# Cross-attention memory keys and values: projected in the second norm of the mixer, or in the band heads of the next block

## The chip, the cores and the metric

One core of one Trainium2 chip runs the whole program. The metric is the device time of one execution in microseconds (us); the time of a version is the median of its runs. Engines are named as the profile names them: PE (TensorE matmuls), PEld (its weight loads), DVE (VectorE), ACT (ScalarE), POOL (GpSimd), SP (SyncE, which only issues DMAs here).

## The reference, cut to what matters

Two blocks follow each other on 512 positions of width 1024 (the first has 16 meta positions ahead of them). The first is a token mixer and a gated feed-forward; the second takes its output through four groups of heads (A dilated, B stick-breaking, C a band of 128 with a learned sink, D block-sparse), a cross-attention into 256 memory tokens, and a squared-ReLU feed-forward. All is float32. What the change touches:

```python
# first block
h = h + rmsnorm(merged @ w_out, g_post)                  # the mixer's second norm
h = rmsnorm(h, g_pre)                                    # channel_mixer
a = causal_dwconv(h @ w_gate, w_conv, b_conv)            # FFN_DIM = 2816
y = (gelu(a) * (h @ w_up)) @ w_down
# second block
x = x + concat(groups) @ w_out                           # hybrid_mixer: heads, then this
kv = rmsnorm_2(mem, g_mem) @ w_kv                        # mem: 256 x 1024, w_kv: 1024 x 512
p = softmax(einsum("bshe,bmhe->bhsm", q, k) * X_SCALE)   # q from x
o = einsum("bhsm,bmhe->bshe", p, v)
```

The memory is an input of its own: its keys and values depend on nothing that the first block computes, and are wanted only by the cross-attention.

## The kernel before, in words

**Products.** Activations lie transposed, eight tiles of 128 features by positions. Every number is held as a high and a low part of a reduced type, and a product is hi·hi + hi·lo + lo·hi: `mm3` (L141) and `product` (L160) issue three matmuls for each of eight 128-row slices, 24 for each range of columns. `weights` (L111) loads 512 KB of float32 through SP's queue into one of three buffers `wst`; ACT writes the high part `whi` (L126) and DVE the low part `wlo` (L127), three buffers each. `split_early` (L130) splits a weight ahead of time: a load on POOL's queue (L135), ACT and DVE for `phi` and `pst` (L105, L106), two stores to DRAM on POOL's queue (L139); `weights(..., ready=...)` then only loads both parts through SP (L119, L120).

**Banks.** `product_bank` (L185) gives accumulators in turn: in `merge` and in the feed-forward from three banks `mx` and two banks `mm`; in the heads from the two `mm` alone. A further bank `rs` is for the norms' factors.

**`merge` (L954)** runs the mixer's output product in two halves of the columns (`TAIL`), eight weights each. Between the eight outputs of the first half `memory_input` (L1582) loads the memory, splits it into tiles `ya`, `yb` that are free by then, and forms its norm's factor. Each half is followed by `post_norm` (L1034), a chain of twelve steps over DVE, ACT and POOL: a factor `prs`, then for each of eight tiles a multiply (L1039, in turn on DVE and on POOL), the residual sum (L1040), the split for the next product (L108, L109) and the square for the next norm (`add_square`, L243; its sums L252 are on POOL), and at its end the next norm's factor `rs` (L287 to L307). The first half's chain is woven between the second half's output products. The second half's chain, the *second norm*, has no output products left beside it, so `zip_steps` (L998) spreads the list `early` between its steps: the two key and two value products of the memory (`memory_keys`, L1602) and the products on the first half of the columns for three feed-forward weights (gate 0, up 0, gate 1), seven products of 24 matmuls with 256 or 258 columns:

```python
load, early = self.chain(self.memory_keys(mem), jobs[0][0])
early.insert(0, load)
jobs[0] = (lambda: None, jobs[0][1])
...
for load, pieces in jobs[0:3]:
    early += [load] + pieces[0:3]
    rest += pieces[3:]
```

Keys and values go to DRAM (`mkd`, `mvd`) by ten POOL DMAs (L1621, L1637) and come back in the cross-attention (`memory_load`, L1640).

**Feed-forward (`ffn_jobs` L1051, `ffn` L1088).** What `early` didn't take is `rest`: second halves, then the other gate and up products. A product's evacuation multiplies by `rs` (`graw` L1062, `up` L1077). Between the pieces seventeen `split_early` prepare weights of the second block.

**The second block's heads (`hybrid`, L1342).** `weave` (L1314) runs the chains of two pairs of heads side by side and puts the jobs of `plan` (L1527) between them: projections for later heads, and at the last two sets, the band heads ("C", 0) and ("C", 1), the first half of the output product: `project_out(f)` for eight f (L1510; 12 matmuls of 512 columns, a weight of 256 KB, and a sum into x). `finish(g)` turns a group's outputs into split inputs. The jobs of a set are placed in order among its units; each job's weight is loaded at the job before it.

**Order.** The framework reorders instructions by its own estimate of times; on the chip each engine, and each engine's DMA queue, takes its instructions in the order that the program then has.

The functions that the diff touches:

Of the kernel before, what the change touches and what calls it, by code (L numbers as in the profile page):

```python
# [11 lines left out]
FT = mybir.dt.float32  # L12
FR = mybir.dt.float32r
# [6 lines left out]
P = 128  # L20
# [43 lines left out]
class Net:  # L64
# [95 lines left out]
    def product(self, src, ranges, evac, m=P, after=None, own=None):  # L160

        nc = self.nc
        st = {}
# [19 lines left out]
        return load, pieces + ([after] if after else [])  # L183

# [769 lines left out]
    def merge(self, mem, mt, yas, ybs, mg, sgs):  # L954
# [93 lines left out]
    def ffn_jobs(self, e2):  # L1048
# [7 lines left out]
        for f in range(NFF):  # L1056
            t = {}

            def gate(ps, t0, n, t=t):
                if "g" not in t:  # L1060
                    t["g"] = ft.tile([P, L], FT, name="graw")
                V.tensor_tensor(t["g"][:, t0:t0 + n], ps, rs[:, t0:t0 + n], OP.mult)  # L1062
# [21 lines left out]
            jobs.append(self.product(I["w_gate"][f], TAIL, gate, after=conv))  # L1084
            jobs.append(self.product(I["w_up"][f], HALF if f < 2 else WHOLE, up, after=end))
        return jobs

    def ffn(self, e2, rest):  # L1088
        nc = self.nc
        I = self.I  # L1090
        with ExitStack() as es:
            self.fp = self.pool(es, "fp")
            self.hid = hid = []
            with ExitStack() as e3:
# [5 lines left out]
                early[11:11] = [("v", 2, c) for c in range(2)]  # L1100
                for i, piece in enumerate(rest):
                    piece()
                    while len(self.ready) < min(len(early), (i + 1) * len(early) // (len(rest) - 20)):
                        key = early[len(self.ready)]
                        self.split_early(pool, key, I["w_in2"][key[1]] if key[0] == "f" else I["w_v2"][key[1], key[2]])
# [236 lines left out]
    def hybrid(self):  # L1342
# [3 lines left out]
        with ExitStack() as es:  # L1346
# [165 lines left out]
            def project_out(f):  # L1512
# [13 lines left out]

            plan = [  # L1527
# [8 lines left out]
                (("C", 0), [(None, [lambda: finish(1), lambda: finish(0)])] + [project_out(f) for f in range(3)]),  # L1536
                (("C", 1), [(None, [lambda: finish(3)])] + [project_out(f) for f in range(3, 6)] + [
# [40 lines left out]
    def memory_input(self, mp):  # L1578
# [5 lines left out]
        self.mem = mh, ml, rm  # L1584
        for k in range(KT):
# [12 lines left out]
    def memory_keys(self, mp):  # L1598
# [3 lines left out]
        mh, ml, rm = self.mem  # L1602
        self.mkd = self.dram.tile([64, 8, MEM], FT, name="mkd")
        self.mvd = self.dram.tile([P, 4, 256], FT, name="mvd")

        def keys(f):
            st = {}

            def load():
                st["w"] = self.weights(I["w_xk"][f], (8, P))  # L1610

            def make():
                ps = self.product_bank()
                self.mm3(ps[:, 0:MEM], self.terms(st["w"], 0, list(zip(mh, ml)), 0, MEM, KT))
                kn = mp.tile([P, MEM], FT, name="kn")
                nc.vector.tensor_tensor(kn, ps[:, 0:MEM], rm, OP.mult)
# [354 lines left out]
```

## Time and profile before

| | |
|---|---|
| runs | 1526.29, 1524.48, 1523.43 us; median 1524.48 |
| profiled execution | 1522.43 us; span 1520.6 us from the first to the last instruction |
| busy in the span | PE 1464.7 us, DVE 1007.9, ACT 741.1, POOL 292.7 |
| mean granted clock of TensorE | 0.993 of full speed |
| DMA | 197.10 MB, mean 130 GB/s |

The span is 1.83 us shorter than its execution's own time. Landmarks of the span, by the lines that run: the second norm is at 441 to 480 us (the memory's products at 441 to 455), the feed-forward's gate and up products follow to about 770, the D heads end and the band heads run at 1000 to 1070, with the output products among them, and the cross-attention follows. A busy time is the sum over an engine's instructions, overlaps counted once; an engine that isn't busy in a stretch waits for another or for data.

### The profile page before, as it was taken

The page shows a single profiled execution, that of the slowest core. Times are in us where ns is not written, and L with a number is a line of the kernel's source. Part 1 is how long each engine was busy: PE and PEld are TensorE (multiplying, and loading weights), DVE is VectorE, ACT ScalarE, POOL GpSimd, SP SyncE. Part 2 cuts the span into 40 slices and gives each one's busy share as a digit, 9 for nine tenths or more (in the row PEclk, how much of TensorE's full clock was granted, in tenths as well). Part 3 has the DMA queues.
Part 4 walks back from the last instruction along what each step waited for, and adds up shares of the span by engine and source line. Part 5 has one row for each costly group of instructions (what it writes and reads, how often), then busy time and mean ns, then how long its engine had stood idle before and what let it go on. Part 6 is the DMA issues. An engine that isn't in the chain of part 4 may idle for free.

```text
span 1520.6 us, 25150 instructions
## 1 busy us (share of the span) xinstructions
PE 1464.7 (96%) x9769; PEld 1320.4 (87%) x9769; DVE 1007.9 (66%) x1963; ACT 741.1 (49%) x1437; POOL 292.7 (19%) x332
## 2 busy tenths in 40 slices
PE   7899899999999999999999999999899999999996
PEld 7899899988989989989999988888888888888885
DVE  6988979877587766655474766798895443344334
ACT  5333357665565444444454465686675431144321
POOL 1157822003363111100141221000221000000001
PEclk9999999999999999999999999999999999999998
DMA  6333332226545766643657344314311332232221
GB/s 207 100 100 95 107 113 77 77 68 224 161 151 199 245 242 224 246 140 116 189 154 244 106 142 138 112 46 143 98 56 58 96 97 97 89 96 94 97 84 56
DMA packets 75087, 197.10 MB, mean 130 GB/s; under 512 B 16076, under 2 KB 24508, under 8 KB 74840
## 3 DMA queue, kind: packets, MB, share of 16 engines
q1 hardware_dynamic: 65816, 165.08, 34.8%
q0 software_dynamic: 8064, 29.36, 5.4%
q8 instruction: 77, 1.26, 0.3%
q10 hardware_dynamic: 1088, 1.05, 0.2%
q14 instruction: 42, 0.34, 0.1%
HBM read 171.75 MB, written 27.63 MB: 131 GB/s over the span
## 4 chain that ended last, share of the span: by engine, by line
PE 62%; DVE 5%; ACT 2%; DMA 1%; issue 0%; DVEq 0%; ACTq 0%
PE mm L146 6%; PE mm L147 6%; PE mm L149 6%; PE mm L176 5%; PE mm L179 5%; PE mm L178 5%; PE mx L179 4%; PE mx L176 4%; PE mx L178 4%; PE mx L146 2%; PE mx L147 2%; PE mx L149 2%; PE mm L1396 2%; PE mm L1395 2%; PE mm L1393 2%; PE tr L1252 1%
## 5 line engine op out<-in xcount | busy, mean ns | idle before, releaser
L127 DVE TENSOR_TENSOR wlo<-wst,whi 128x1024 fp32r<-128x1024 f32 (+3 forms) x244 | 299.9, 1230 | 192.7 <-ACT whi L126 117.9
L126 ACT ACTIVATE whi<-wst 128x1024 fp32r<-128x1024 f32 (+3 forms) x244 | 249.9, 1026 | 269.7 <-PE mm L147 112.6
L178 PE MATMUL mm<-xh,whi 128*128 128x256 f32 (+4 forms) x784 | 225.6, 313 | 3.2 <-DVE u L762 2.1
L179 PE MATMUL mm<-xl,whi 128*128 128x256 f32 (+4 forms) x784 | 226.4, 314 | 0.3 <-DVE xl L109 0.2
L178 PE MATMUL mx<-xh,whi 128*128 128x512 f32 (+3 forms) x592 | 178.1, 324 | 7.4 <-ACT xh L108 7.2
L179 PE MATMUL mx<-xl,whi 128*128 128x512 f32 (+3 forms) x592 | 178.8, 325 | 0.6 <-DVE xl L109 0.6
L178 PEld LDWEIGHTS mm<-xh,whi 128*128 128x128 f32 (+1 forms) x784 | 148.1, 189 | 13.5 <-DVE u L762 2.5
L179 PEld LDWEIGHTS mm<-xl,whi 128*128 128x128 f32 (+1 forms) x784 | 147.7, 188 | 11.0 <-DVE xl L109 0.7
L176 PE MATMUL mm<-xh,wlo 128*128 128x256 f32 (+4 forms) x784 | 135.6, 312 | 0.6 <-DVE wlo L127 0.6
L146 PE MATMUL mm<-hh,whi 128*128 128x256 f32 (+1 forms) x480 | 132.7, 307 | 0.0
L147 PE MATMUL mm<-hl,whi 128*128 128x256 f32 (+1 forms) x480 | 132.6, 307 | 0.0
L178 PEld LDWEIGHTS mx<-xh,whi 128*128 128x128 f32 x592 | 112.1, 189 | 16.3 <-ACT xh L108 7.2
L176 PEld LDWEIGHTS mm<-xh,wlo 128*128 128x128 f32 (+1 forms) x784 | 113.1, 187 | 10.7 <-DVE wlo L127 0.8
L179 PEld LDWEIGHTS mx<-xl,whi 128*128 128x128 f32 x592 | 111.8, 189 | 10.7 <-DVE xl L109 1.5
L176 PE MATMUL mx<-xh,wlo 128*128 128x512 f32 (+3 forms) x592 | 107.5, 323 | 0.0
L176 PEld LDWEIGHTS mx<-xh,wlo 128*128 128x128 f32 x592 | 88.8, 189 | 9.0
L146 PEld LDWEIGHTS mm<-hh,whi 128*128 128x128 f32 x480 | 90.4, 189 | 5.4
L147 PEld LDWEIGHTS mm<-hl,whi 128*128 128x128 f32 x480 | 90.5, 189 | 5.1
L252 POOL TENSOR_TENSOR nacc<-nacc,sq 128x256 f32<-128x256 f32 (+2 forms) x58 | 56.4, 972 | 196.9 <-ACT sq L251 191.1
L149 PE MATMUL mm<-hh,wlo 128*128 128x256 f32 (+1 forms) x480 | 79.6, 307 | 1.3 <-DVE wlo L127 1.3
L149 PEld LDWEIGHTS mm<-hh,wlo 128*128 128x128 f32 x480 | 67.5, 188 | 6.7 <-DVE wlo L127 1.7
L252 POOL TENSOR_TENSOR acc<-acc,sq 128x264 f32<-128x264 f32 (+1 forms) x6 | 4.3, 739 | 335.3 <-ACT sq L251 335.3
(589 smaller groups left out, 3316.3 us busy)
## 6 DMA issues: line engine op xcount, KB each, us to landing
wst<-in_w_in_dram SPq DMA_DIRECT2D x39, 512.0 KB, 3.6
wst<-in_w_down_dram SPq DMA_DIRECT2D x32, 512.0 KB, 3.5
wst<-in_w_mup_dram SPq DMA_DIRECT2D x32, 512.0 KB, 3.6
wst<-in_w_mdown_dram SPq DMA_DIRECT2D x32, 512.0 KB, 3.7
wst<-in_w_gate_dram SPq DMA_DIRECT2D x22, 512.0 KB, 3.6
wst<-in_w_up_dram SPq DMA_DIRECT2D x22, 512.0 KB, 3.6
wst<-in_w_out_dram SPq DMA_DIRECT2D x20, 512.0 KB, 4.4
ready<-phi POOLq DMA_DIRECT2D x17, 512.0 KB, 3.3
```

The source lines that it names most:

```text
L126: nc.scalar.activation(hi[:, 0:n], st[:, 0:n], AF.Copy)
L127: nc.vector.tensor_tensor(lo[:, 0:n], st[:, 0:n], hi[:, 0:n].bitcast(FT), OP.subtract)
L146: nc.tensor.matmul(ps, ah, bh, start=start and i == 0, stop=False)
L147: nc.tensor.matmul(ps, ah, bl, start=False, stop=False)
L149: nc.tensor.matmul(ps, al, bh, start=False, stop=stop and i == n - 1)
L176: nc.tensor.matmul(ps, wl[:, k], xh, start=False, stop=k == KT - 1)
L178: nc.tensor.matmul(ps, wh[:, k], xh, start=k == 0, stop=False)
L179: nc.tensor.matmul(ps, wh[:, k], xl, start=False, stop=False)
L252: (nc.vector if k % len(accs) else nc.gpsimd).tensor_tensor(acc[:, c:c + w], acc[:, c:c + w], sq, OP.add)
L1393: nc.tensor.matmul(ps, wl[:, k], xh, start=False, stop=k == KT - 1)
L1395: nc.tensor.matmul(ps, wh[:, k], xh, start=k == 0, stop=False)
L1396: nc.tensor.matmul(ps, wh[:, k], xl, start=False, stop=False)
```

## The change

`memory_input` stores the memory's split tiles and its factors to DRAM (eight DMAs of 256 KB and two small ones, on POOL's queue). `memory_keys` no longer takes part in `merge`; in the heads ("C", 0) its `inputs` loads the tiles back on POOL's queue into the activations' tiles xh4 to xh7 and xl4 to xl7, `factors` the factors, and two key and two value products follow with weights that four more `split_early` have prepared at the end of the feed-forward. Their results lie in tiles of the values' pool instead of buffers of their own. One output product stays in ("C", 0), the others go to ("C", 1). In the second norm, `early` holds the first halves of five feed-forward weights: up 1, gate 2, gate 0, up 0, gate 1. For gate 0, up 0 and gate 1 the second halves go on with the same split weight, as before; for up 1 and gate 2 `product_twice` gives each half a load of its own, so that weight is loaded and split a second time for its second half. `graw` gets three buffers.

```diff
+    def product_twice(self, src, ranges, evac, after):
+        st = {}
+        a, b = (self.product(src, [r], evac, after=after if i else None, held=st) for i, r in enumerate(ranges))
+        return a[0], b[0], a[1] + b[1]
...
         jobs = self.ffn_jobs(e2)
-        load, early = self.chain(self.memory_keys(mem), jobs[0][0])
+        first, jobs = jobs[0:5], jobs[5:]
+        load, early = self.chain([(a, pieces[0:3]) for a, _, pieces in first[3:] + first[0:3]])
         early.insert(0, load)
-        jobs[0] = (lambda: None, jobs[0][1])
-        rest = []
-        for load, pieces in jobs[0:3]:
-            early += [load] + pieces[0:3]
-            rest += pieces[3:]
-        load, pieces = self.chain(jobs[3:])
+        rest = [piece for _, _, pieces in first[0:3] for piece in pieces[3:]]
+        load, pieces = self.chain([(b, pieces[3:]) for _, b, pieces in first[3:]] + jobs)
...
-                    t["g"] = ft.tile([P, L], FT, name="graw")
+                    t["g"] = ft.tile([P, L], FT, name="graw", bufs=3)
...
+                early += [(n, c) for n in ("w_xk", "w_xv") for c in range(2)]
...
+            inputs, factors, mem = self.memory_keys()
...
-                (("C", 0), [(None, [lambda: finish(1), lambda: finish(0)])] + [project_out(f) for f in range(3)]),
-                (("C", 1), [(None, [lambda: finish(3)])] + [project_out(f) for f in range(3, 6)] + [
+                (("C", 0), [(None, [inputs, lambda: finish(1), lambda: finish(0), factors]), project_out(0)] + mem),
+                (("C", 1), [(None, [lambda: finish(3)])] + [project_out(f) for f in range(1, 6)] + [
...
+            if k % 2:
+                for x in range(2):
+                    nc.gpsimd.dma_start(self.mem[0][x, k // 2], pair[x][:, 0:512].bitcast(FT))
             yield
         yield from self.rstd_steps(mp, rm, macc, MEM)
-        self.mcol = self.r
+        nc.gpsimd.dma_start(self.mem[1][:, 0:MEM], rm)
+        nc.gpsimd.dma_start(self.mem[1][:, MEM:MEM + 2], self.r)
...
+        def inputs():
+            for k in range(4):
+                for x, halves in enumerate((mh, ml)):
+                    d = self.act.tile([P, L], FR, name=f"x{'hl'[x]}{k + 4}")
+                    nc.gpsimd.dma_start(d[:, 0:512].bitcast(FT), self.mem[0][x, k])
+                    halves += [d[:, 0:MEM], d[:, MEM:512]]
+            t.extend(self.vp.tile([P, 4, 256], FR, name=f"v2{x}") for x in "hl")
+
+        def factors():
+            m["r"] = self.nrm.tile([P, L], FT, name="rs", bufs=2)
+            nc.gpsimd.dma_start(m["r"][:, 0:MEM + 2], self.mem[1])
...
-                st["w"] = self.weights(I["w_xk"][f], (8, P))
+                st["w"] = self.weights(None, (8, P), ready=self.ready["w_xk", f])
```

## Rows read from the trace of the kernel before

**Rows 1.** Page, part 1: busy us (share of the span) xinstructions.

```profile
PE 1464.7 (96%) x9769; PEld 1320.4 (87%) x9769; DVE 1007.9 (66%) x1963; ACT 741.1 (49%) x1437; POOL 292.7 (19%) x332
```

**Rows 2.** Stretches: us, busy PE, PEld, DVE, ACT, POOL; PEclk, DMA share, GB/s.

```profile
360.00:370.00 10.00, 10.00 (x86) 10.00 (x85) 9.11 (x18) 4.17 (x10) 6.11 (x6) 1.00 1.01 336
441.00:455.00 14.00, 13.51 (x114) 13.32 (x113) 11.19 (x25) 7.71 (x17) 9.50 (x8) 1.00 0.76 244
455.00:470.00 15.00, 13.94 (x111) 13.12 (x110) 13.92 (x21) 8.30 (x17) 10.72 (x17) 1.00 0.41 128
...
500.00:700.00 200.00, 200.00 (x1285) 181.57 (x1284) 130.37 (x176) 86.59 (x103) 22.48 (x42) 1.00 0.60 207
1000.00:1030.00 30.00, 28.40 (x212) 24.74 (x211) 29.07 (x102) 24.58 (x71) 0.00 (x0) 1.00 0.16 49
1030.00:1050.00 20.00, 20.00 (x118) 17.22 (x117) 14.40 (x51) 11.81 (x36) 0.00 (x0) 1.00 0.51 163
1050.00:1070.00 20.00, 16.40 (x117) 13.14 (x117) 19.16 (x72) 16.43 (x57) 0.00 (x0) 1.00 0.31 93
1070.00:1090.00 20.00, 18.92 (x145) 18.09 (x145) 15.95 (x32) 12.43 (x29) 6.60 (x7) 0.92 0.25 80
```

**Rows 3.** PE in order of time: start us, us, line, operation, count.

```profile
425.33 1.11 PE L149 MATMUL mx<-r,wlo 128*128 128x256 f32 x8
...
1031.58 1.10 PE L149 MATMUL mm<-xh,wlo 128*128 128x512 f32 x4
```

**Rows 4.** PE groups, 1000 to 1070 us: busy us, mean ns, idle before.

```profile
L146 PE MATMUL mm<-xh,whi 128*128 128x512 f32 x32 | 12.6, 403 | 0.8 <-ACT xh L105 0.8
...
L1252 PE MATMUL tr<-ptl,v2h 128*64 128x128 f32 x19 | 4.1, 222 | 0.0
```

**Rows 5.** Groups of DVE by shape, 441 to 480 us.

```profile
L127 DVE TENSOR_TENSOR wlo<-wst,whi 128x1024 fp32r<-128x1024 f32 x10 | 13.0, 1312 | 3.4 <-ACT whi L126 3.3
...
L109 DVE SCALAR_TENSOR_TENSOR vl<-mx,rsr,vh 128x256 fp32r<-128x256 f32 x1 | 0.5, 472 | 0.0
...
L1616 DVE TENSOR_TENSOR kn<-mx,rm 128x256 f32<-128x256 f32 x1 | 0.4, 418 | 0.0
```

**Rows 6.** Waits, 441 to 480 us: us in total, times, longest.

```profile
ACT sq L251 <- POOL nacc L252: 5.0, 3, 4.1
...
ACT phi L105 <- DMA pst<-in_w_in_dram: 3.3, 1, 3.3
...
POOL mvd L1637 <- DVE vl L109: 2.9, 1, 2.9
...
ACT kh L105 <- DMA mkd<-kh: 2.1, 1, 2.1
```

**Rows 7.** Groups of DVE by shape, 1000 to 1070 us.

```profile
L127 DVE TENSOR_TENSOR wlo<-wst,whi 128x512 fp32r<-128x512 f32 x5 | 3.4, 685 | 0.0
```

**Rows 8.** DMA issues: queue, count, KB each, median us to landing.

```profile
pst<-in_w_in_dram POOLq DMA_DIRECT2D x13, 512.0 KB, 4.7
...
bias<-ed SPq DMA_DIRECT2D x16, 256.0 KB, 3.0
...
xv<-mvd POOLq DMA_DIRECT2D x1, 512.0 KB, 7.9
```

**Rows 9.** PE in order of time: last projection, first output product.

```profile
994.73 1.79 PE L1393 MATMUL mm<-xh,wlo 128*128 128x512 f32 x7
...
1008.97 0.70 PE L146 MATMUL mm<-xh,whi 128*128 128x512 f32 x2
```

**Rows 10.** POOL in order of time: the loads of keys and values.

```profile
1090.60 1.11 POOL L1645 DMA_DIRECT2D xk<-mkd  x2 [2.12 <-PE rs L290]
```

**Rows 11.** Line 1039: ns min/median/max, first and last start.

```profile
L1039 POOL TENSOR_TENSOR sga<-sga,prs x8: 633/874/4371, 420.9 to 455.7; 128x258 f32<-128x258 f32 x4, 128x256 f32<-128x256 f32 x4
```

**Rows 12.** Groups of POOL, 441 to 480 us.

```profile
L1621 POOL DMA_DIRECT2D mkd<-kh x4 | 2.4, 590 | 4.1 <-ACT kh L105 4.1
```

**Rows 13.** Line 307, a factor's end: ns min/median/max, first and last start.

```profile
L307 ACT ACTIVATE rs<-rs x2: 385/386/387, 453.0 to 480.0; 128x258 f32<-128x258 f32 x1, 128x256 f32<-128x256 f32 x1
```

More of the change, by code (lines that the diff above doesn't have):

```diff
@@ L158, in project, with product @@
             evac(ps[0:m, 0:n], t0, n)
-    def product(self, src, ranges, evac, m=P, after=None, own=None):
+    def product(self, src, ranges, evac, m=P, after=None, own=None, held=None):
         nc = self.nc
-        st = {}
+        st = {} if held is None else held
         def load():
@@ L1083, in end @@
                 self.hid.append((hi, lo))
-            jobs.append(self.product(I["w_gate"][f], TAIL, gate, after=conv))
-            jobs.append(self.product(I["w_up"][f], HALF if f < 2 else WHOLE, up, after=end))
+            jobs.append(self.product_twice(I["w_gate"][f], TAIL, gate, conv) if f < 3 else
+                        self.product(I["w_gate"][f], TAIL, gate, after=conv))
+            jobs.append(self.product_twice(I["w_up"][f], HALF, up, end) if f < 2 else
+                        self.product(I["w_up"][f], WHOLE, up, after=end))
         return jobs
@@ L1583, in memory_input @@
         rm = mp.tile([P, MEM], FT, name="rm")
-        self.mem = mh, ml, rm
+        self.mem = self.dram.tile([2, 4, P, 512], FT, name="memd"), self.dram.tile([P, MEM + 2], FT, name="rmd")
         for k in range(KT):
@@ L1614, in make, with values @@
                 self.mm3(ps[:, 0:MEM], self.terms(st["w"], 0, list(zip(mh, ml)), 0, MEM, KT))
-                kn = mp.tile([P, MEM], FT, name="kn")
-                nc.vector.tensor_tensor(kn, ps[:, 0:MEM], rm, OP.mult)
-                ks = [mp.tile([P, MEM], FR, name=t) for t in ("kh", "kl")]
-                self.split(*ks, kn)
+                kl, kh = (x[:, 2 + f] for x in t)
+                kn = kl.bitcast(FT)
+                nc.vector.tensor_tensor(kn, ps[:, 0:MEM], m["r"][:, 0:MEM], OP.mult)
+                self.split(kh, kl, kn)
                 for j in range(2):
-                    for x in range(2):
-                        nc.gpsimd.dma_start(self.mkd[:, 4 * f + 2 * j + x], ks[x][64 * j:64 * j + 64].bitcast(FT))
+                    for x, half in enumerate((kh, kl)):
+                        nc.gpsimd.dma_start(self.mkd[:, 4 * f + 2 * j + x], half[64 * j:64 * j + 64].bitcast(FT))
             return load, [make]
-        v = [mp.tile([P, 2, 256], FR, name=n) for n in ("vh", "vl")]
-        ws = []
         def load():
-            ws.extend(self.weights(I["w_xv"][c], (4, 256)) for c in range(2))
-        def values(t):
+            ws.extend(self.weights(None, (4, 256), ready=self.ready["w_xv", c]) for c in range(2))
+        def values(i):
             ps = self.product_bank()
-            sl = slice(t * P, t * P + P)
+            sl = slice(i * P, i * P + P)
             self.mm3(ps[:, 0:256], [(mh[k][:, sl], ml[k][:, sl], ws[k // 4][0][:, k % 4, :],
                                      ws[k // 4][1][:, k % 4, :]) for k in range(KT)])
-            self.split(v[0][:, t, :], v[1][:, t, :], ps[:, 0:256], self.mcol[:, t:t + 1])
-            if t == 1:
-                for i in range(2):
-                    nc.gpsimd.dma_start(self.mvd[:, 2 * i:2 * i + 2], v[i].bitcast(FT))
-        return [keys(0), keys(1), (load, [lambda t=t: values(t) for t in range(2)])]
+            self.split(t[0][:, i], t[1][:, i], ps[:, 0:256], m["r"][:, MEM + i:MEM + i + 1])
+            if i == 1:
+                for x in range(2):
+                    nc.gpsimd.dma_start(self.mvd[:, 2 * x:2 * x + 2], t[x][:, 0:2].bitcast(FT))
+        return inputs, factors, [keys(0), keys(1), (load, [lambda i=i: values(i) for i in range(2)])]
     def memory_load(self, pool):
```

8 lines of the change are left out of this document (5 added, 3 removed).

## The prediction, made before the changed kernel ran

> **What bounds the kernel.** The page's first part comes first: PE is busy 96% of the span and DVE 66% [rows 1], so time comes mostly from PE work or from PE gaps. The second view is the table of stretches [rows 2]. From 500 to 700 us, the feed-forward, PE is busy all 200.00 us: a matmul taken out there is time won. From 441 to 470 us, the second norm, PE misses 1.55 us (29.00 less 13.51 and 13.94) while DVE is busy 25.11. From 1000 to 1070 us, the end of the D heads and the band heads, PE misses 5.20 us (1.60, 0 and 3.60), where DVE is busy 29.07 of 30.00 and 19.16 of 20.00: there PE waits for VectorE. The third view is the order in time, for spacing [rows 3]: eight 256-column matmuls take 1.11 us, the last of them 0.28 as every single one does, so one starts 0.119 us after another; four of 512 columns take 1.10, the last 0.40, so 0.233. A busy PE thus hides slack, and I count as well. From 1000 to 1070 us there are 447 starts by the three rows. The eight output products, 12 matmuls each, are 96 of them at 512 columns [rows 4], 22.4 us; 57 have 128 columns (three rows of 19, one is shown), at half of 0.119, 3.4 us; the other 294 at 0.119 make 35.0. That is 60.8 of 70 us, so the slack lies between 5.2 and 9.2 us.
>
> **The change part by part, and the sum.** *Memory products.* Two key and two value products of 24 matmuls, 96 x 0.119 = 11.4 us of PE, move from the norm to the heads. *Half products.* Two more feed-forward halves, 48 matmuls, move from the feed-forward into the norm, 5.7 us. PE's total work is unchanged; what counts is its idle time.
>
> *Feed-forward: -5.7 us*, since PE is full there. Its additions (two weights loaded and split again, four more early splits with three POOL issues each) lie beside that full PE, with DVE at 130.37 and POOL at 22.48 of 200: nothing. If that cover went, six splits at 1.31 us [rows 5] would be 8 us.
>
> *Norm: PE work falls by 11.4 - 5.7 = 5.7 us.* How much of it is time depends on the norm's own chain on DVE, which the fill only just covers. The change takes from it two kn, two kl of the same size and two vl (0.42, 0.42 and 0.47 us each: 2.6) and two of the ten wlo splits (2.6), and adds two evacuations the size of kn (0.8) [rows 5]: 4.4 us shorter. Waits that the memory put there go too: ACT for a key's store 2.1 us, POOL for vl 2.9, and part of ACT's 5.0 behind POOL's sums [rows 6]; they overlap the DVE work, so I count none. With 5.7 less work in front of a chain 4.4 shorter, the stage shrinks by 4.4 and 1.3 becomes idle. Bounds: a chain not shorter at all (5.7 idle), and one so short that the 1.55 us of before go as well.
>
> *Heads: +11.4 us of PE work, less the slack it fills.* Fill finds slack only if its matmuls are ready when DVE keeps PE waiting. I take the 5.2 us that the table shows as idle, because the rest is gaps inside busy stretches: +6.2. Bounds: nothing filled (+11.4), all 9.2 filled (+2.2). On DVE the evacuations (2.6 us) come in, but two output products leave the first band heads for the second, and with them two 512-column splits of 0.69 us [rows 7] and two sums of that width; 1030 to 1050 us has 5.6 us of DVE free. The granted clock of 1070 to 1090 is 0.92, so some 3 us of it lay at 1.2 instead of 2.4 GHz, after PE had been busy 16.40 of 20.00; if fuller heads keep the high level, up to 1.6 us come back, not counted.
>
> *Queues.* The ten stores of keys and values go from a POOL that the norm needs to one that is busy 0.00 of 70 us: free, and so are the issues of the eight input loads and of the factor. Behind the merge's splits, ten POOL issues (5.5 us) and 2.1 MB of writes are new, where 360 to 370 us already moves 336 GB/s at a full share; 2.1 MB is 6 us at that rate, and the next weights stand behind it. PE is 10.00 of 10.00 there, on branch products: I take 0, bound 6. SP gets eight loads of ready weights in the heads; one that waits for a weight buffer holds a bias tile behind it (3.0 us to land [rows 8]) and the unit that reads it: 0 taken, bound 3.
>
> *Sum:* -5.7 - 4.4 + 6.2 = -3.9 us. The profiled execution took 1522.43 us, so 1518.5 by it; it lies 2.05 below the median of the runs, 1524.48, so on their scale 1520.5.
>
> **The rivals.** *A, more slack than idle.* The heads fill all 9.2 us and the clock stays high: -10.1 + 2.2 - 1.6 = -9.5, 1515.0. For it: DVE leaves 5.6 us free in 1030 to 1050, and PE 3.60 afterwards. Against it: PE executes in order, and gaps of some 0.1 us are not found by whole products.
>
> *B, the heads grow one for one.* Every matmul of fill goes ahead of a head's, DVE starves as in 1030 to 1050 (PE 20.00 of 20.00, DVE 14.40), and nothing is filled: -10.1 + 11.4 = +1.3, 1525.8. For it that row; against it the idle on both sides of it.
>
> *C, slower: PE stands in front of the first key product.* Its inputs come back from DRAM on POOL's queue, into tiles that the last projection reads until 996.5 us [rows 9]. The nearest row is the three loads of 0.5 MB from 1090.60 on [rows 10], issued 0.55 us apart, the last landing 7.9 us after its issue [rows 8]: 1.57 MB in 9 us. So 2.1 MB takes 12 us and lands by 1009, when the first output product begins [rows 9], some 3 us before PE comes to the keys: no wait. If DVE holds POOL back as in the norm, where a multiply of 0.63 us at the shortest took 4.37 [rows 11], twofold is landing at 1021: PE stands 9 us with the heads behind it, -3.9 + 9 = +5, 1529.5. The kernel is slower if it lands after 1019. The Trainium skill, SBUF — State Buffer, section SBUF: two separate sides, says that GpSimd writes the descriptors of a DMA from its queue and is locked out while VectorE holds the port pair they share; by that rule these loads come late under the busy VectorE of the heads, and the result is this rival's time. The trace speaks against it so far: with DVE busy 11.19 of 14.00 us a store took 0.59 us of POOL [rows 12], and POOL's loads in the feed-forward land in 4.7 [rows 8].
>
> *D, the norm is uncovered.* The second half's factor came at 480.0 us [rows 13], and now five second halves instead of three wait for it in five banks. If it stays there, PE runs out of work after ten halves, and norm and feed-forward win only the 48 matmuls done earlier: -5.7 + 6.2 = +0.5, 1525.0. For it: ACT waits 3.3 us for an early load just before that factor [rows 6], and early splits now come closer together. Against it: the memory's waits on POOL are gone.
>
> That the products don't land where the text puts them is possible for single instructions only: their loads bind them to weights and tiles.
>
> **How the numbers follow.** Forecast 0.48, A 0.12, B 0.18, C 0.13, D 0.09. A measurement of this kernel tells about 0.2%, 3.05 us, from no change. The forecast lies close to that bound: of its 0.48 I put 0.05 inside (slack filled of under 4.3 us). So faster 0.43 + 0.12 = 0.55; same 0.05 + 0.18 + 0.09 = 0.32; slower 0.13, C alone. The range reaches from a little past A (1514) to beyond B and D and into C's smaller waits (1528); it leaves out most of C and the edge of A, under 2 in 10.
>
> **What would show it.** Right: from 500 us on a full PE as before, the feed-forward ending some 10 us earlier; in the norm no kn, no store of keys, and 1 to 3 us of PE idle; between the last projection and the first cross product clearly less PE idle than 5.2 us, less free time on DVE in the middle, and the stage some 6 us longer. Wrong: a PE wait of several us on xh or on ready weights in the heads (C), free DVE time grown there with PE's slack unchanged (B), a PE wait on a bank or on rs after the norm (D), or weights that come late in the merge.

## The result, and the profile after

The changed kernel takes 1535.43 us (median of 6 runs, 1532.69 to 1537.05) against 1523.95 for the kernel before (6 runs, 1518.45 to 1526.36) on the same chip: a ratio of 1.0086 with an interval of 1.007 to 1.0102. It is slower by 11.5 us, where 4 us less was forecast. Its profiled execution took 1535.69 us, with a span of 1534.0 and a mean granted clock of 0.988 of full speed. The page's first part, against [rows 1]:

```profile
PE 1467.3 (96%) x9769; PEld 1324.5 (86%) x9769; DVE 1009.2 (66%) x1965; ACT 741.4 (48%) x1439; POOL 304.0 (20%) x363
```

The work is the same: as many matmuls, 2.6 us more of PE, 31 more POOL instructions. So the 13.3 us between the two spans are almost all idle time, a slower clock and an end that is longer. To find them, the span is cut at instructions that both kernels have: the evacuation of the last output product of the merge, DVE's last multiply that joins a gate with an up product (707.8 us before, not the 770 of the landmarks), the evacuation of the last down product, a factor after the D heads (the second `rs` of 512 columns after 1000 us), the first sum into x in the function `cross` (the second half of the heads' output product, with which the cross-attention's code begins), and the last DVE instruction. Lengths in us:

| stage, up to | before | after | difference |
|---|---|---|---|
| last output product of the merge | 444.93 | 448.24 | +3.3 |
| last gate times up (norm and feed-forward) | 262.88 | 260.80 | -2.1 |
| last down product | 125.37 | 127.83 | +2.5 |
| factor after the D heads | 184.95 | 182.91 | -2.0 |
| first sum into x in `cross` (band heads) | 56.14 | 66.84 | +10.7 |
| last DVE instruction | 441.57 | 440.02 | -1.5 |
| end of the span | 4.81 | 7.35 | +2.5 |

Kernels whose code for a stage is the same differ in that stage by some 2 us from one execution to the next, and by up to 3 in the long stage up to the merge's end (see the table of all runs below), so a difference of this size is not read here without a row that shows its cause. The first such rows are stretches, columns as in [rows 2]. The first fence is the kernel before, the second the changed kernel:

```profile
350.00:360.00 10.00, 9.09 (x66) 8.08 (x65) 8.75 (x21) 5.89 (x12) 3.56 (x4) 1.00 0.59 180
444.93:499.93 55.00, 53.45 (x411) 51.06 (x411) 45.58 (x79) 31.89 (x55) 23.45 (x30) 1.00 0.62 213
444.93:707.81 262.88, 261.33 (x1737) 239.47 (x1737) 180.55 (x261) 121.74 (x162) 45.92 (x72) 1.00 0.60 204
```

```profile
350.00:360.00 10.00, 5.90 (x45) 5.44 (x44) 4.91 (x13) 3.61 (x8) 2.41 (x4) 0.92 0.65 217
360.00:370.00 10.00, 10.00 (x65) 10.00 (x66) 10.00 (x17) 4.87 (x11) 6.44 (x10) 0.73 0.88 308
448.24:503.24 55.00, 47.01 (x330) 44.90 (x331) 38.68 (x68) 28.04 (x49) 20.38 (x27) 0.91 0.63 219
448.24:709.04 260.80, 252.81 (x1647) 231.60 (x1648) 177.15 (x254) 119.21 (x159) 44.49 (x72) 0.98 0.62 211
1000.00:1030.00 30.00, 29.49 (x235) 27.28 (x234) 27.84 (x97) 22.87 (x67) 5.82 (x12) 1.00 0.57 201
1050.00:1070.00 20.00, 20.00 (x126) 17.47 (x125) 16.17 (x58) 12.57 (x36) 0.00 (x0) 1.00 0.57 180
1070.00:1090.00 20.00, 16.00 (x116) 13.44 (x115) 14.34 (x43) 13.13 (x39) 0.73 (x1) 0.91 0.08 27
```

Three things are to be seen. At 350 to 360 us, in the merge, PE misses 4.10 us (0.91 before) and then runs at a granted clock of 0.73, where before it was full at 1.00 [rows 2]. The norm ends 3.3 us later in the changed kernel, so it is compared from the merge's last evacuation on: of the next 55 us PE misses 7.99, against 1.55 before, at a clock of 0.91 against 1.00. The rows of the whole stage miss no more than that, so the feed-forward behind is as full as before. In that stage PE's busy time falls by 8.5 us (261.33 to 252.81) and its idle time rises by 6.4: that is the 2.1 us that the stage became shorter. In the heads the idle time that stood at 1050 to 1070 before (3.60, [rows 2]) now stands 20 us later, at 1070 to 1090 (4.00). The waits of PE in the merge, 335 to 395 us, and in the norm, 425 to 500 us, name the releasers (us in total, times, longest):

```profile
PE mx L146 <- ACT whi L126: 4.1, 1, 4.1
```

```profile
PE mm L178 <- DVE graw L1066: 6.0, 1, 6.0
PE mm L274 <- POOL acc L1033: 2.8, 1, 2.8
```

**The merge.** ACT makes the high parts of the merge's weights, and it takes its instructions in order. Its timeline from 356 us shows what stood ahead of the `whi` that PE waited for: the split of a memory tile, which itself waited 4.86 us for the tile's load.

```profile
357.23 0.51 ACT L108 ACTIVATE ya<-mem,par 128x256 fp32r<-128x256 f32 x1 [4.86 <-DMA mem<-in_mem_dram]
...
358.65 1.99 ACT L126 ACTIVATE whi<-wst 128x1024 fp32r<-128x1024 f32 x2
```

SP's timelines from 351 us, the kernel before first and then the changed one, show that load at nearly the same moment, 352.09 and 351.92. But in the changed kernel one of the twelve copies of bias tiles (`ed<-gd`, 320 KB) has slipped ahead of it, and the data is used at 357.23 instead of 354.51.

```profile
352.09 0.83 SPq L1587 DMA_DIRECT2D mem<-in_mem_dram  x2
353.03 1.84 SPq L1149 DMA_DIRECT2D ed<-gd  x3
```

```profile
351.25 0.57 SPq L1157 DMA_DIRECT2D ed<-gd  x1
351.92 1.01 SPq L1596 DMA_DIRECT2D mem<-in_mem_dram  x2
```

**The norm.** The early splits moved forward: the first one's load is issued at 417.17 us (468.27 before), the second's at 432.30, and the second's stores then stand in POOL's order in the middle of the norm. In all six kernels of the before line the first load is issued between 467.5 and 473.7 us, five halves or three; so the move goes with the memory's projections. That it is because the memory's tiles come free earlier is likely, but was not tested apart. POOL's timeline, 417 to 419 and 441 to 449 us:

```profile
417.17 0.56 POOL L135 DMA_DIRECT2D pst<-in_w_in_dram  x1
```

```profile
445.36 0.53 POOL L139 DMA_DIRECT2D ready<-pst  x1 [3.55 <-DVE pst L106]
445.91 2.02 POOL L1033 TENSOR_TENSOR acc<-acc,osq 128x256 f32<-128x256 f32 x1
```

The second store waits 3.55 us for DVE's half of the split. Behind it wait the sum of squares `acc`, which PE needs for the norm's first factor, and the last sums `nacc` for the next norm's factor (they end at 451.95 us, before at 443.37). That factor, `rs` of the first half of the columns, comes at 465.9 us, where before it came at 453.0 [rows 13]. The row of its line, 441 to 490 us:

```profile
L313 ACT ACTIVATE rs<-rs x2: 363/374/384, 465.9 to 487.9; 128x258 f32<-128x258 f32 x1, 128x256 f32<-128x256 f32 x1
```

From the merge's last evacuation that is 17.7 us instead of 8.1 (465.9 less 448.24; 453.0 less 444.93). The five halves hold the five banks, and from 465.5 us on PE stands 6.0 us for `graw`. The factor is there at 466.3, after 0.8 of them. The larger part comes behind it: DVE runs the second half's chain first and evacuates the first of the half products only at 470.62. DVE's rows, before (the norm's last splits) and after:

```profile
464.79 2.71 DVE L109 SCALAR_TENSOR_TENSOR xl<-x,par,xh 128x256 fp32r<-128x256 f32 x3
```

```profile
467.70 3.00 DVE L109 SCALAR_TENSOR_TENSOR xl<-x,par,xh 128x256 fp32r<-128x256 f32 x5
470.62 0.41 DVE L1081 TENSOR_TENSOR up<-mx,rs 128x256 f32<-128x256 f32 x1
...
472.29 1.13 DVE L109 SCALAR_TENSOR_TENSOR xl<-x,par,xh 128x256 fp32r<-128x256 f32 x2
```

The last of these splits ends the norm's chain on DVE: 22.6 us after the merge's last evacuation before (464.79 + 2.71 less 444.93), 25.2 in the changed kernel (472.29 + 1.13 less 448.24).

**The heads.** The same two stages cut by the instructions named above, D heads and then band heads, first before and then after, columns as in the stretches:

```profile
833.17:1018.12 184.95, 181.93 (x1179) 162.29 (x1180) 134.92 (x340) 114.61 (x284) 27.91 (x44) 1.00 0.36 117
1018.12:1074.26 56.14, 51.50 (x334) 43.79 (x334) 46.80 (x163) 38.78 (x122) 0.00 (x0) 0.97 0.34 104
```

```profile
836.87:1019.78 182.91, 180.63 (x1177) 162.15 (x1177) 132.36 (x334) 111.86 (x276) 32.87 (x53) 1.00 0.40 141
1019.78:1086.62 66.84, 62.84 (x433) 55.43 (x432) 53.09 (x176) 43.99 (x131) 5.37 (x10) 0.97 0.42 134
```

PE has 97 more matmuls recorded and is busy 10.04 us longer (180.63 + 62.84 less 181.93 + 51.50). Its idle time falls from 3.02 + 4.64 = 7.66 us to 2.28 + 4.00 = 6.28: 1.4 us of the idle time was filled, and the two stages together grow by 8.7. The loads of the memory's tiles were no part of it: they were issued from 996.8 us on and landed within 8.4 us, and under "who waited for it" nothing stands.

```profile
L1625 POOL DMA_DIRECT2D xl<-memd x4: 546/552/584, 996.8 to 998.5; - x4
L1625 POOL DMA_DIRECT2D xh<-memd x4: 546/546/548, 999.3 to 1001.1; - x4
...
who waited for it (us, times):
...
DMA to landing us min/median/max: 3.6/7.3/8.4
```

**The end.** After its last operation each engine drains. POOL's drain is the last thing in the span, and it is 2.5 us longer. The row of the program's last line, before and after; the third number is the longest of three drains, in ns:

```profile
L1966 POOLq DRAIN  x3: 46/93/7169, 1512.7 to 1520.4; - x3
```

```profile
L1991 POOLq DRAIN  x3: 51/93/9704, 1523.5 to 1533.7; - x3
```

### The profile page after: what moved, and what is told of

Read it like the earlier page. It is cut to its first block, busy times and chain, and to the rows that moved or that the text cites. A ratio compares the mean times of both kernels' runs of the same rounds, so it can differ in the third digit from the quotient of the medians.

```text
span 1534.0 us, 25247 instructions
## 1 busy us (share of the span) xinstructions
PE 1467.3 (96%) x9769; PEld 1324.5 (86%) x9769; DVE 1009.2 (66%) x1965; ACT 741.4 (48%) x1439; POOL 304.0 (20%) x363
## 4 chain that ended last, share of the span: by engine, by line
PE 61%; DVE 6%; ACT 1%; DMA 1%; issue 0%; DVEq 0%; ACTq 0%
PE mm L146 6%; PE mm L147 6%; PE mm L149 6%; PE mm L178 5%; PE mm L179 5%; PE mm L176 5%; PE mx L176 4%; PE mx L179 4%; PE mx L178 4%; PE mx L146 2%; PE mx L147 2%; PE mx L149 2%; PE mm L1404 2%; PE mm L1403 2%; PE mm L1401 2%; PE tr L1260 1%
## 5 line engine op out<-in xcount | busy, mean ns | idle before, releaser
L258 POOL TENSOR_TENSOR nacc<-nacc,sq 128x256 f32<-128x256 f32 (+2 forms) x58 | 52.5, 906 | 121.0 <-ACT sq L257 117.1
```

The costliest lines, as they stand in the source:

```text
L258: (nc.vector if k % len(accs) else nc.gpsimd).tensor_tensor(acc[:, c:c + w], acc[:, c:c + w], sq, OP.add)
```

## The experiments

Eleven kernels were run, each timed in several runs beside the kernel before. Their stages, cut in the same places (profiled executions, us), with the number of DMAs that POOL issues in the program and the time from POOL's last operation to the end of its drain:

| kernel | merge | norm, feed-forward | down | D heads | band heads | rest | end | POOL DMAs | drain |
|---|---|---|---|---|---|---|---|---|---|
| before | 444.93 | 262.88 | 125.37 | 184.95 | 56.14 | 441.57 | 4.81 | 64 | 5.31 |
| halves_only | 446.61 | 264.24 | 126.21 | 184.97 | 54.59 | 440.49 | 4.81 | 64 | 5.31 |
| before_bias | 446.53 | 263.53 | 126.47 | 185.04 | 55.20 | 439.45 | 4.81 | 64 | 5.31 |
| before_ends | 449.59 | 263.64 | 126.66 | 184.76 | 61.75 | 441.81 | 4.81 | 64 | 5.31 |
| one_store | 443.62 | 282.12 | 125.34 | 185.39 | 54.65 | 440.74 | 3.57 | 47 | 3.93 |
| drain96 | 445.98 | 295.83 | 123.20 | 186.53 | 55.14 | 439.83 | 3.67 | 160 | 4.17 |
| after | 448.24 | 260.80 | 127.83 | 182.91 | 66.84 | 440.02 | 7.35 | 95 | 7.84 |
| stores_late | 452.11 | 261.05 | 127.88 | 183.41 | 65.38 | 439.44 | 7.35 | 95 | 7.84 |
| splits_late | 451.00 | 255.46 | 128.43 | 183.06 | 65.27 | 440.17 | 7.35 | 95 | 7.85 |
| bias_pinned | 446.57 | 257.34 | 126.82 | 182.95 | 66.79 | 440.05 | 7.35 | 95 | 7.84 |
| outs_late | 449.18 | 257.05 | 127.50 | 182.63 | 67.51 | 439.44 | 7.35 | 95 | 7.85 |
| memory_only | 449.62 | 256.38 | 127.74 | 182.62 | 66.24 | 440.96 | 7.35 | 95 | 7.84 |
| outs_end | 447.41 | 257.49 | 126.32 | 183.21 | 73.44 | 442.87 | 7.55 | 95 | 7.84 |

**splits_late: the changed kernel, the first early split kept in its place.**

```diff
-        nc.gpsimd.dma_start(st, src)
+        ld = nc.gpsimd.dma_start(st, src)
+        if len(self.ready) == 1:
+            self.tc.keep_in_program_order(ld)
```

> The changed kernel, with the first early split's load held behind the norm's last POOL work in POOL's queue. Theory (the splits came forward): once the memory's tiles are free at 416 us, early splits run from 417 instead of 468 us, and their stores stand in POOL's queue ahead of the sums that the norm's chain needs. Without them the factor of the first half (rs) comes by 457 instead of 465.9, PE's idle time from 425 to 500 us falls from 10.9 to 6 or less, and the kernel takes about 1530 (5 us less). Rival (the first halves wait for the factor in their five banks, whatever the splits do): the 6 us wait on the bank stays, 1534 to 1536.

Measured: 1532.73 us (1530.11 to 1534.28), 1.0067 [1.0053, 1.0082] of the kernel before. Norm and feed-forward take 255.46 us, 5.3 less than in the changed kernel. The wait for `acc` is gone, and the factor comes 9.7 us after the merge's last evacuation (460.7 less 451.00) instead of 17.7. The theory was right in kind but not in full: it had the factor by 457, and PE's idle time from 425 to 500 us at 6 or less, where 10.9 became 7.1. The row of the factor, PE's wait from 425 to 500 us, the 55 us behind the merge's last evacuation, and two rows of DVE:

```profile
L315 ACT ACTIVATE rs<-rs x2: 366/375/384, 460.7 to 486.8; 128x258 f32<-128x258 f32 x1, 128x256 f32<-128x256 f32 x1
```

```profile
PE mm L180 <- DVE graw L1068: 2.5, 2, 1.3
```

```profile
451.00:506.00 55.00, 50.93 (x366) 48.13 (x365) 41.37 (x72) 28.89 (x50) 15.46 (x20) 0.97 0.52 174
```

```profile
464.78 0.41 DVE L1083 TENSOR_TENSOR up<-mx,rs 128x256 f32<-128x256 f32 x1
...
467.50 3.17 DVE L109 SCALAR_TENSOR_TENSOR xl<-x,par,xh 128x256 fp32r<-128x256 f32 x5
```

So the forward move of the splits is shown as the cause of the late factor, at some 3 to 5 us of the stage (255.5 to 257.5 us in the five kernels that have this edit, 260.8 and 261.1 in the two of the changed line that have not). PE still misses 4.07 us, 2.5 more than before. The factor is not what it waits for now: that was there at 461.0 us, PE stops at 464.4, and DVE evacuates the first of the half products at 464.78, behind the sums of the second half's chain. The second of the two waits, from 486.8 on, is for products that need the second half's factor, which comes at that moment. The norm's chain on DVE ends 19.7 us after the merge's last evacuation (467.50 + 3.17 less 451.00).

**stores_late: the changed kernel, the memory's stores written after its factor.**

```diff
+                pairs.append(pair)
...
+        for i, pair in enumerate(pairs):
+            for x in range(2):
+                nc.gpsimd.dma_start(self.mem[0][x, i], pair[x][:, 0:512].bitcast(FT))
```

> The changed kernel, with the eight stores of the memory's tiles issued after the memory's last step instead of after each pair. Theory (the stores slow the memory's loads, ACT waits for them with a weight's split behind): PE's wait of 4.1 us near 355 us goes, the merge's first evacuation comes some 4 us earlier, and the kernel takes about 1531.5. Rival (the load is late because of the bias copies ahead of it in SP's queue): the wait stays, 1535.

Measured: 1536.35 us, 1.009 [1.0075, 1.0104]; PE's wait in the merge is 4.6 us instead of 4.1. This run separates little: the framework placed the stores on POOL from 349.5 to 383.5 us, nearly where they were (345.6 to 379.2), so the edit did not do what it was for, and the theory that the stores slow the loads is left to bias_pinned.

**drain96: the kernel before, with 96 stores of 1 KB on POOL's queue in the feed-forward.**

```diff
+                junk = self.dram.tile([96, P, 2], FT, name="junk")
...
+                        self.tc.keep_in_program_order(nc.gpsimd.dma_start(junk[j], self.ones[:, 0:2]))
```

> The kernel before, with 96 stores of 1 KB each on POOL's queue beside the full PE of the feed-forward. Theory (POOL's last drain takes 0.0825 us for each DMA that its queue had: 5.31 us after its last operation with 64 of them, 7.84 with 95): 160 DMAs make 13.2 us, so the kernel takes some 7.9 us longer than before, 1532. Rival (it goes by bytes or by descriptors of data, or the drain hides something else): the drain stays within 1 us of 5.3 and the time within 1 us of before.

Measured: 1552.71 us, 1.0192 [1.017, 1.0213]. Its end is 1.1 us *shorter* than before, not longer: neither the theory (13.2 us) nor the rival (within 1 us of 5.3, and no change of the time). So the number of POOL's DMAs in the whole program does not set the drain by itself. Two rows bear on it: the drain, and a stop of POOL of 2.23 us that the profile puts down to issue, ahead of the 118th of its 160 DMAs.

```profile
L1969 POOLq DRAIN  x3: 46/93/6029, 1543.4 to 1549.9; - x3
```

```profile
675.39 1.61 POOL L1105 DMA_DIRECT2D junk<-ones  x3 [2.23 <-issue]
```

The feed-forward became 33 us longer, which no theory had; that is told at the end.

**halves_only: the kernel before, with five halves in the norm, the memory's products still there.** The edit is the changed kernel's `product_twice` and its lists, with `memory_keys(mem)` left ahead of the halves:

```diff
+        first, jobs = jobs[0:5], jobs[5:]
+        load, early = self.chain(self.memory_keys(mem) + [(a, pieces[0:3]) for a, _, pieces in first[3:] + first[0:3]])
```

> The kernel before, with five first halves instead of three behind the memory's products in the second norm; the memory's projections stay there. Theory (the memory's products cover the norm because they need no factor): no bank wait over 2 us in the norm, the feed-forward is 5.7 us shorter, the norm longer by 5.7 less what it fills of its 6 us of slack: 1519 to 1524. Rival (five first halves in five banks stall wherever they stand): a PE wait of 3 us or more on an evacuation, 1525 to 1529.

Measured: 1523.7 us, 1.0009 [0.9998, 1.0019]; norm and feed-forward 1.4 us longer, with 3.05 us of PE idle behind the merge's last evacuation instead of 1.55. No wait for a bank shows, so the rival is out, but the 5.7 us are not there either: the two halves more bring nothing.

**bias_pinned: splits_late, with the copies of the bias tiles kept in their place on SP.**

```diff
+        self.tc.keep_in_program_order(
+            self.nc.sync.dma_start(self.ed[h], bass.AP(tensor=row.tensor, offset=row.offset, ap=[[0, P], [1, 640]])))
```

> The run splits_late (1532.7 us), with the twelve bias copies held at their places in the feed-forward, where the program lists them, instead of in SP's queue beside the memory's loads. Theory (a bias copy stands ahead of the memory's load in SP's queue, so that load lands 5 us after its issue instead of 2.4, and ACT holds a weight's split behind it): PE's wait of 4.4 us in the merge goes, 1528 to 1529. Rival (the memory's stores on POOL's queue slow the load): the wait stays, 1532 to 1533.

Measured: 1530.04 us, 1.0046 [1.0029, 1.0063], the best of the changed line. PE's wait for that `whi` falls from 4.4 us in splits_late to 0.5. Two waits come in that splits_late doesn't have there, so not all of it is won; PE's waits from 335 to 395 us:

```profile
PE mm L148 <- DVE sga L954: 1.3, 1, 1.3
PE mx L151 <- DVE wlo L127: 1.0, 1, 1.0
PE mx L148 <- ACT whi L126: 0.5, 1, 0.5
```

The merge takes 446.6 and 447.4 us in the two kernels of the changed line with the copies pinned, 448.2 to 452.1 in the five without. The memory's stores are in all of them. So the wait goes with the copies in SP's queue, and not with the stores' 2.1 MB of writes. All twelve copies left that place at once: that it is the one ahead of the load is read from the two orders, and was not tested alone. (The interval of the time overlaps that of splits_late; the wait is what shows it.)

**outs_late: splits_late, with the output products from the fourth on kept in their place in the heads.**

```diff
+            mm = nc.tensor.matmul(ps, ah, bh, start=start and i == 0, stop=False)
+            if late and i == 0:
+                self.tc.keep_in_program_order(mm)
...
-                    self.mm3(ps, [(wh[:, k], wl[:, k], *out[k]) for k in (2, 3, 0, 1)])
+                    self.mm3(ps, [(wh[:, k], wl[:, k], *out[k]) for k in (2, 3, 0, 1)], late=f >= 3)
```

> The run splits_late, with the output products 3 to 7 of the band heads held at their places in the program's order instead of as early as they are ready. Theory (fill runs ahead of the heads, so that it is used up when the last units of the band leave PE idle, and the memory's products lengthen the stage one for one): from the second factor after the D heads to the first product of the cross-attention 65.3 us become 61 to 63, total 1529 to 1531. Rival (the chain of the units is no shorter with fill beside its end): 65 us or more, 1532 to 1535.

Measured: 1532.91 us, 1.0069 [1.0051, 1.0086], as splits_late. The band heads take 67.51 us. PE has 1.80 us idle in their last 18 us instead of 4.01 in the last 21, but 2.27 in the 40 us ahead, which were full: the idle moved, and none of it was filled. The rival had it so.

**memory_only: splits_late with three halves, as before the change.** The memory's products are gone from the norm and nothing is put in their place.

```diff
-        load, early = self.chain([(a, pieces[0:3]) for a, _, pieces in first[3:] + first[0:3]])
+        load, early = self.chain([(a, pieces[0:3]) for a, pieces in jobs[0:3]])
```

> The run splits_late, with the three first halves of before in the norm instead of five. Theory (the halves are what fills the place of the memory's products): from the last output evacuation of the merge to the last feed-forward gate, 262.9 us before and 255.5 in splits_late, 259 to 261 us, since 5.7 us of products come back behind a norm that is no shorter; total 1536 to 1538. Rival (the memory's leaving alone shortens the norm, the halves only trade places): 255 to 257, 1532 to 1534.

Measured: 1532.12 us, 1.0061 [1.0045, 1.0077], as the rival had it. Norm and feed-forward take 256.38 us, in the midst of the kernels with five halves and the splits held (255.46 to 257.49). The 55 us behind the merge's last evacuation, and the norm's last splits on DVE:

```profile
449.62:504.62 55.00, 51.20 (x358) 48.06 (x357) 44.06 (x75) 28.50 (x50) 13.86 (x20) 0.94 0.52 170
```

```profile
462.45 4.76 DVE L109 SCALAR_TENSOR_TENSOR xl<-x,par,xh 128x256 fp32r<-128x256 f32 x7
```

PE misses 3.80 us here, and 4.07 with five halves. The chain on DVE ends 17.6 us after the merge's last evacuation (462.45 + 4.76 less 449.62), where with five halves it ends at 19.7. So the two halves give PE work, but the chain that the work is to cover ends later with them.

**one_store: the kernel before, with one store for both parts of an early split.** Same bytes, 47 POOL DMAs instead of 64.

```diff
+        two = pool.tile([P, 2, 1024], FR, name="phi")
+        st = two[:, 1].bitcast(FT)
...
-        for i, t in enumerate((hi, lo)):
-            nc.gpsimd.dma_start(d[i], t.bitcast(FT))
+        nc.gpsimd.dma_start(d.rearrange("a p c -> p a c"), two.bitcast(FT))
```

> The kernel before, with both parts of an early split stored by one DMA on POOL's queue instead of two: 47 DMAs there instead of 64, the same bytes. Theory (the last drain of POOL's queue takes 0.083 us for each DMA, as long as their number stays under some 110): 3.9 us after POOL's last operation instead of 5.3, and 1.4 us less in all, 1522. Rival (it goes by bytes): 5.3 us.

Measured: 1539.51 us, 1.0116 [1.0093, 1.0139]. The end is 1.24 us shorter:

```profile
L1966 POOLq DRAIN  x3: 46/93/5788, 1528.7 to 1535.1; - x3
```

So the theory's drain came as it said, but not its 1522 us. 47, 64 and 95 DMAs give 3.93, 5.31 and 7.84 us after POOL's last operation: 0.081 a DMA between the first two (1.38 over 17), 0.082 between the others (2.53 over 31), for the same bytes in the first two. The feed-forward lost 19 us, since one buffer now holds the input, its high and its low part until the single store is done, and load, split and store follow one another. Waits from 500 to 720 us:

```profile
POOL phi L136 <- DMA ready<-phi: 66.9, 14, 5.5
...
PE mm L178 <- DVE graw L1062: 10.8, 5, 2.5
```

**outs_end, before_ends, before_bias: can the end of the band heads be filled?** outs_end is bias_pinned, before_ends the kernel before with the bias copies pinned; both hold back the output products as outs_late does and put the last two behind the heads' last units. before_bias is the kernel before with the bias copies pinned alone.

```diff
+            for f in (6, 7):
+                load, steps = project_out(f)
+                load()
+                steps[0]()
```

> The run bias_pinned (1530.0 us), with the last two output products behind the last unit of the band heads and the others from the fourth on held in the program's order. Theory (the idle time of the heads lies in their last 20 us, when nothing is left to fill it): from the second factor after the D heads to the first product of the cross-attention 66.8 us become 62 to 64, total 1525 to 1528. Rival (that end is a chain through DVE and ACT, and the products only move their place): 66 us or more, 1529 to 1532.

> The kernel before, with the bias copies held in the feed-forward and the output products held as in outs_end. Theory: 56.1 us from the factor to the cross-attention become 52 to 54, total 1519 to 1521. Rival: 56 us or more, 1522 to 1525.

> The kernel before, with the twelve bias copies held at their places in the feed-forward. Theory (in the kernel before, the memory's load stood ahead of the copies in SP's queue and PE waited less than 1 us for a weight there): the merge gains 0 to 1 us, the feed-forward's full PE hides the copies, total 1522 to 1524. Rival (the copies cost the weights of the feed-forward time): 1525 or more.

Measured: 1537.51 us, 1.0093 [1.008, 1.0107], for outs_end; 1534.46, 1.0072 [1.0059, 1.0086], for before_ends; 1526.4, 1.0025 [1.0013, 1.0036], for before_bias. In both lines the band heads become 6.6 us longer (73.44 against 66.79, 61.75 against 55.20). For the stage the rivals had it so; in time both kernels are slower than even they said. The rows of the stage, bias_pinned and then outs_end:

```profile
1013.69:1080.49 66.80, 62.79 (x433) 55.40 (x432) 53.11 (x176) 44.01 (x131) 5.39 (x10) 0.97 0.43 133
```

```profile
1014.42:1087.86 73.44, 67.01 (x446) 57.52 (x445) 55.59 (x177) 47.59 (x137) 5.39 (x10) 0.95 0.40 122
```

PE's idle time rises from 4.01 to 6.43 us, and 1.64 of it lies at 1040 to 1060 us, where bias_pinned has none: what was taken from the middle is missing there. The other 4.2 us are busy time, with 13 more matmuls recorded in the stage and a granted clock of 0.95 instead of 0.97. A reading of this is that the heads are a chain over PE, ACT and DVE that runs at its own pace; it is shown for these three placements only. Pinning the copies alone makes the kernel before 0.25% slower, as its rival had it: it mends only what the change had disturbed.

No version beats the kernel before.

## Why the prediction was wrong

**The sum, term by term.** Forecast: feed-forward -5.7, norm -4.4, heads +6.2, queues 0, sum -3.9. Measured in the profiled executions: norm and feed-forward together -2.1, heads +8.7, merge +3.3, end +2.5, and +0.9 in down products and rest together: +13.3.

**Norm and feed-forward (-10.1 forecast, -2.1 measured).** The step that failed is "with 5.7 less work in front of a chain 4.4 shorter, the stage shrinks by 4.4 and 1.3 becomes idle". The chain did not become shorter: on DVE it ends 25.2 us after the merge's last evacuation instead of 22.6. And PE's idle time rose by 6.4 us (1.55 to 7.99), not by 1.3, with the clock down to 0.91 over those 55 us. There are two causes.

- The larger is a place that the sum took as fixed. The text asked for the price of the early splits that are added, and found that they "lie beside that full PE" and cost nothing. The splits that did the harm were not added ones: the first of the seventeen old ones moved 51 us forward, into the norm, on the engines whose order the norm depends on. With it held (splits_late), the chain ends at 19.7, PE's idle time is 4.07, and the stage becomes 7.4 us shorter instead of 2.1; in the four kernels with five halves and this hold it is 5.4 to 7.4. That is 3.3 to 5.3 of the missing 8.0 us.
- The rest is the term for the halves, -5.7. "A matmul taken out there is time won" holds for the feed-forward, where PE is full, but it was paid in the norm, where the matmuls went. Without the two halves the stage is 6.5 us shorter (memory_only), as much as with them, and beside the memory's products they win nothing (halves_only, 1.4 us longer). With the splits held, the chain on DVE is 2.0 to 2.9 us shorter than before with five halves and 5.0 with three: the halves' weights are split and their products evacuated on the same DVE. That this is why they bring nothing is a reading of DVE's order, not tested apart.

Rival D had the place and half of the mechanism (PE out of work, halves waiting in five banks), but a sum of +0.5, much too small a price. It named the second half's factor. In the changed kernel it was the first half's, late by 13 us, and behind it DVE's order; the second half's shows in splits_late, as a wait of 1.3 us.

**The heads (+6.2 forecast, +8.7 measured).** The mis-sized term is the slack that the fill would find: 5.2 us taken, 2.7 measured (11.4 less 8.7). Of it 1.4 is idle time (7.66 before, 6.28 after, between the last down product and the first sum in `cross`). The other 1.3 lies inside busy stretches, since PE's busy time grew by 10.0 us and not by 11.4; the text had seen such gaps, and left them out of its sum. The text said itself that fill finds slack only if its matmuls are ready when DVE keeps PE waiting, and then took the idle of a stretch as fillable. Of the idle, 3.60 us lay at 1050 to 1070 [rows 2], behind the last output product; the new fill ended ahead of such a tail too. So the heads came out about midway between the forecast and rival B, one for one. Three ways of moving fill to that tail (outs_late, outs_end, before_ends) made the heads' idle time no smaller.

**Queues (0 taken).** POOL and SP in the heads were free, as said: no PE wait on ready weights or on the memory's tiles. The merge's +3.3 lies inside the bound of 6 us, but for another reason than the one named. The 2.1 MB of writes cost nothing that shows; what shows is a wait of 4.1 us that goes with the bias copies in SP's queue, one of which moved past the memory's load, while ACT stood behind that load with a `whi` behind it. What made the framework change this order was not tried apart from the change.

**The end (not in the sum).** The last 2.5 us are POOL's drain. The prediction counted every DMA that was moved or added, but looked for its price only where it was issued.

**The slower side** had chance 0.13, all of it with rival C, and C did not happen: loads in by 1009.5 us at the latest (1001.1 + 8.4), as the forecast's "no wait" had it, with DVE busy 27.84 of 30 us. The rule of the Trainium skill (SBUF — State Buffer, section SBUF: two separate sides) that was cited with C was not seen to bind here: these loads' issues took 0.546 to 0.584 us each on POOL under that DVE. The rule is for the time in which VectorE holds the shared port pair, and no run shows whether the operations of the heads hold it. What did make the kernel slower were two orders that the framework wrote anew, work that found less idle time than was taken, and a term at the end.

**What stays open:** the down products are 2.5 us longer in the changed kernel, of which 1.4 is a new PE wait on a factor (`rs` behind DVE's `rc`); kernels of the line before spread from 125.3 to 126.7 there (drain96 lies at 123.2), those of the changed line from 126.3 to 128.4, and no run took that apart. Why POOL's drain is short in drain96 is open too.

## What to carry to other kernels

Fill is not counted in matmuls alone: ask of each piece what it must wait for, and on which engine its weight's split and its evacuation stand, since fill for PE can lengthen the very chain that it is to cover. An idle time is slack for moved work only if work can stand at that place; an idle tail behind the last filler stays one. When a change frees buffers early, look at every in-order queue for what will start early because of it, and compare the order of the issues before and after, above all on the queues that the change does not mean to touch. When two kernels are compared stretch by stretch, start the stretches at the same instruction, not at the same microsecond.

## What was not expected of the hardware

- POOL's drain at the end of the program grew with the DMAs on its queue: 3.93, 5.31 and 7.84 us for 47, 64 and 95, so about 0.08 us each; the bytes were the same for the first two. With 160 it was 4.17, after a stop of POOL of 2.23 us in the middle of the program; that the drain counts only from some such stop is an argument, not shown, and no run shows a number of DMAs from which on it stops growing.
- 96 stores of 1 KB (128 rows of 8 bytes) made the feed-forward 33 us longer: while they ran, weights of 512 KB on SP's queue landed in 7.8 and 9.2 us. The issues of 500 to 700 us in drain96, and then before (median us to landing, last):

```profile
wst<-in_w_up_dram SPq DMA_DIRECT2D x17, 512.0 KB, 7.8
wst<-in_w_gate_dram SPq DMA_DIRECT2D x16, 512.0 KB, 9.2
```

```profile
wst<-in_w_gate_dram SPq DMA_DIRECT2D x16, 512.0 KB, 3.6
wst<-in_w_up_dram SPq DMA_DIRECT2D x16, 512.0 KB, 3.6
```

- A wait of PE can cost more than itself. After the 4.10 us missing at 350 to 360 us the granted clock of the next 10 us was 0.73, a mixture of the levels 1.2 and 2.4 GHz; PE was busy 10.00 of them with 65 matmuls, where before it did 86 at 1.00 [rows 2]. Not every wait does: at 425 to 445 us before, two gaps left 3.02 us missing of 20, and the clock stayed at 1.00.
